# Merge-gate stores issued from GpSimd's queue instead of ScalarE's while attention runs: a hybrid attention and RG-LRU block

## The chip, the cores and the metric

The kernel runs on one core of a Trainium2 chip. The metric is the device time of one execution in microseconds (us); a set of runs is given by its median. The engines are named as in the profile: PE (TensorE), PEld (its weight loads), DVE (VectorE), ACT (ScalarE), POOL (GpSimd) and SP (SyncE, which only issues DMAs here).

## The reference

One decoder block on 1,024 tokens of width 1,024, in float32. An input projection is cut into the inputs of two branches and their gates; each branch is projected back, and two sigmoid gates (`m_attn`, `m_rnn`) merge them:

```python
mod = c @ w_ada[l] + b_ada[l]
shift, scale, gate = jnp.split(mod, 3, axis=-1)
h = rmsnorm(x, norm_g[l]) * (1.0 + scale[:, None, :]) + shift[:, None, :]
proj = h @ w_in[l]
q, k, v, g_attn, xr, g_rnn, m_attn, m_rnn = jnp.split(proj, SPLIT_POINTS, axis=-1)
q = partial_rope(q.reshape(B, S, N_HEADS, HEAD_DIM), positions)
k = partial_rope(k.reshape(B, S, N_KV_HEADS, HEAD_DIM), positions)
v = v.reshape(B, S, N_KV_HEADS, HEAD_DIM)
y_attn = sliding_window_attention_with_sinks(q, k, v, attn_sinks[l]) * jax.nn.silu(g_attn)
xr = causal_depthwise_conv(xr, conv_w[l], conv_b[l])
y_rnn = rg_lru(xr, positions, rg_wa[l], rg_ba[l], rg_wx[l], rg_bx[l], rg_lambda[l]) * jax.nn.silu(g_rnn)
merged = (jax.nn.sigmoid(m_attn) * (y_attn @ w_attn_proj[l])
          + jax.nn.sigmoid(m_rnn) * (y_rnn @ w_rnn_proj[l]))
x = x + gate[:, None, :] * (merged @ w_out[l])
return rmsnorm(x, final_g)
```

The attention has 16 query heads, 4 key heads, a window of 128 and a learned sink per head. The kernel makes each sigmoid as (tanh(z/2) + 1)/2, so what it stores of a merge gate is a tanh.

## The kernel before, in words

**Number format.** Every float32 matrix is split into a high part (rounded to fp32r, a cast on ACT, line 102) and the rest (a subtraction on DVE, line 108); a product is three matmuls: high by high, low by high, high by low.

**The input projection.** It is done in *pairs* of 128-column chunks (class `Pair`), each with seven block products instead of eight (a Strassen-like scheme). A product is 12 matmuls on a bank of PSUM (line 672, tiles `bk`), and fills one *slot* of the hand-written order. `Pair.place` puts every accompanying step into a slot: weight loads (`r<-w_main` by SP), casts (ACT), sums and rests (DVE), and the *sinks*, which take a result block to its place. The list `pairs` ends with the four pairs `MR`, the columns of `m_rnn`. Their sinks come from `tanh_sinks` (lines 768 to 787): ACT takes the tanh of a 128x512 block into a buffer of tag `c` (five of them, line 775), and the buffer is stored to the DRAM tensor `smr_d`, 256 KB a store. `MA`, the columns of `m_attn`, goes the same way to `sma_d`, long before attention.

**Attention over the last pair.** `N_ATT = 1`: when the last pair but one has been placed, `W["att"]` is set (line 1532) and the loop of lines 1563 to 1604 begins. Its round u handles a quarter group of heads for 128 queries, in 32 rounds and three to drain. In PE's order a round is `scores(u)` (8 matmuls into the one buffer `s_ps`, line 1216), then a *piece* (`piece()`: the 12 matmuls of one projection slot while pairs last, 12 matmuls `rp` of the recurrent branch's projection, line 171, afterwards), then `values(u-3)` (line 1288, `pv`, four matmuls, or two where no mask is needed) and `transposed(u-2)` (line 1254, `pt`). ACT copies the scores out of PSUM (line 1224), takes four exponentials (line 1240), does the piece's casts and tanhs, then copies `ob` (lines 1297, 1298) and casts `phc` (line 1259). DVE overlays the masked part (line 1230, which also reads `s_ps` for the last time), takes the maxima (line 1235), scales (lines 1246, 1247), does the piece's rests and joins (lines 108, 732, 743), joins the values (lines 1308, 1309, tile `yq`), and makes `plc` (line 1265). GpSimd issues the loads `dv` and `vs` (line 1195 on), copies the sinks (line 1204) and masks `phc` and `plc` into `phm` and `plm` (line 1274). Line 1433 (tile `al`) writes the low part of the gated attention result into memory that earlier buffers, the `c` buffers among them, held.

**What sets the order.** From line 183 to line 1620 (`order.close()`) all five engines run in the order in which the code is written. Behind that a planner orders the end (the attention projection from line 1652 on, the merge, the output projection) by its own costs. Between engines, the framework places the semaphore waits. Two of its habits matter here: the DMAs issued by SP and by ACT take turns, in the order of the program, on eight completion semaphores, and a DMA whose turn falls on a semaphore waits, on the engine that issues it, until the DMA that used it before (eight such DMAs earlier, by either engine) has landed; GpSimd's DMAs take turns on eight semaphores of their own.

**Stores by other engines.** `store` (line 757) puts a store off to the end of the pieces while `W["att"]` is set and gives it to SP; the merge gates' stores of line 777 do not pass through it.

Of the kernel before, what the change touches and what calls it, by code (L numbers as in the profile page):

```python
# [48 lines left out]
SL = [slice(0, HALF), slice(HALF, S)]  # L49
# [3 lines left out]
def tile_hybrid_block(ctx, tc, x, x_t, pk, rows, posr, posi, c_row, w_ss, w_gate, w_main, w_v,  # L53
                      w_g, w_ap, w_rp, w_out, out):
    nc = tc.nc
    V, A, G, T = nc.vector, nc.scalar, nc.gpsimd, nc.tensor

    def dma(dst, src, eng=nc.sync):
        dst, src = (a.bitcast(F32) if a.dtype == F32R else a for a in (dst, src))
        return eng.dma_start(dst, src)  # L60
# [497 lines left out]
    W = {}  # L558
# [18 lines left out]
    def blk(w=HALF):  # L577
        return stp.tile([P, HALF], F32, tag="c", name="c", bufs=5)[:, :w]
# [178 lines left out]
    def store(dst, src):  # L757

        if "att" in W:
            behind.append(lambda: dma(dst, src))  # L760
        else:
            dma(dst, src)
# [5 lines left out]
    def tanh_sinks(dst, silu):  # L768
        def steps(j, th):
            def sink(s):  # L770
                t = {}

                def f1():
                    t["t"] = blk()
                    A.activation(t["t"], s(), AF.Tanh, scale=0.5)  # L775
                    if not silu:
                        dma(dst[j][:, SL[th]], t["t"], A if "att" in W else nc.sync)

                def f2():
                    V.scalar_tensor_tensor(out=t["t"], in0=t["t"], scalar=1.0, in1=s(),  # L780
                                           op0=ALU.add, op1=ALU.mult)
                    store(dst[j][:, SL[th]], t["t"])

                return [("A", 0.62, 0, f1)] + ([("D", 0, 0.69, f2)] if silu else [])
            return sink
        return {"C11": steps(0, 0), "C12": (blk, steps(0, 1)), "C21": steps(1, 0),
                "C22": (blk, steps(1, 1))}
# [874 lines left out]
    for c in range(KC):  # L1662
# [11 lines left out]
        t = tpool.tile([P, S], F32, tag="tt", name="tt", bufs=2)  # L1674
# [175 lines left out]
```

## Time and profile before

| What | Value |
|---|---|
| Median of three runs | 932.46 us (929.82, 932.46, 933.45) |
| The profiled execution | 932.08 us |
| Its span, first to last instruction | 929.9 us |
| Mean granted TensorE clock | 0.998 |
| Busy: PE, DVE, ACT, POOL | 901.1, 681.1, 533.2, 85.5 us |
| DMA moved | 168.39 MB, mean 181 GB/s |

Times in the profile's rows are microseconds from the start of the span, durations of one instruction are in us in the timeline and in ns where a group is summed up. A row of the timeline gives the start, the duration, engine, line, operation, output and inputs; the bracket at its end gives the engine's idle time just before and what released it. Instructions that only issue a DMA (engine names with a q: ACTq, SPq) do not count as busy time, except on POOL, whose DMAs are shown with the time that GpSimd spends on them. PE's instructions overlap, so what PE loses is read from start to start.

### The profile page before, as it was taken

The page shows a single profiled execution, that of the slowest core. Times are in us where ns is not written, and L with a number is a line of the kernel's source. Part 1 is how long each engine was busy: PE and PEld are TensorE (multiplying, and loading weights), DVE is VectorE, ACT ScalarE, POOL GpSimd, SP SyncE. Part 2 cuts the span into 40 slices and gives each one's busy share as a digit, 9 for nine tenths or more (in the row PEclk, how much of TensorE's full clock was granted, in tenths as well). Part 3 has the DMA queues.
Part 4 walks back from the last instruction along what each step waited for, and adds up shares of the span by engine and source line. Part 5 has one row for each costly group of instructions (what it writes and reads, how often), then busy time and mean ns, then how long its engine had stood idle before and what let it go on. Part 6 is the DMA issues. An engine that isn't in the chain of part 4 may idle for free.

```text
span 929.9 us, 12279 instructions
## 1 busy us (share of the span) xinstructions
PE 901.1 (97%) x4217; PEld 745.5 (80%) x4217; DVE 681.1 (73%) x1042; ACT 533.2 (57%) x1026; POOL 85.5 (9%) x146
## 2 busy tenths in 40 slices
PE   3999999999999999999999999999999999999997
PEld 1679888887888888888887887788888888888886
DVE  5986888888769964996677675799999737657422
ACT  5643655454567656775596784788888622213211
POOL 0110000000000000000000001354454300000000
PEclk9999999999999999999999999999999999999999
DMA  9952548862332541444145349897656186536311
GB/s 350 414 187 102 194 152 281 304 232 85 114 110 94 180 161 36 145 164 154 57 141 187 99 173 294 298 335 219 221 178 189 57 317 219 163 123 242 136 68 68
DMA packets 82148, 168.39 MB, mean 181 GB/s; under 512 B 12756, under 2 KB 29140, under 8 KB 82087
## 3 DMA queue, kind: packets, MB, share of 16 engines
q1 hardware_dynamic: 78596, 159.47, 50.0%
q0 software_dynamic: 2192, 6.00, 1.9%
q10 hardware_dynamic: 1298, 2.15, 0.6%
q8 instruction: 33, 0.54, 0.3%
q14 instruction: 29, 0.23, 0.1%
HBM read 118.20 MB, written 49.78 MB: 181 GB/s over the span
## 4 chain that ended last, share of the span: by engine, by line
PE 87%; DVE 7%; DMA 3%; issue 1%; ACT 1%; SPq 0%; POOL 0%; ACTq 0%; DVEq 0%
PE bk L672 43%; PE rp L171 12%; PE pmain L171 6%; PE rp L1713 5%; PE pgate L966 5%; PE pmain L1713 4%; PE bk L171 3%; PE s_ps L1216 2%; PE pv L1288 2%; DVE jk L248 1%; PE pt L1254 1%; DMA wada<-w_ss 1%; DMA ks<-k_d 1%; PE bk L1461 1%; PE bk L1460 1%
## 5 line engine op out<-in xcount | busy, mean ns | idle before, releaser
L672 PE MATMUL bk<-nh,wl 128*128 128x512 f32 x352 | 137.3, 390 | 0.4 <-DVE wl L108 0.4
L672 PE MATMUL bk<-nh,wh 128*128 128x512 f32 x352 | 137.1, 389 | 0.0
L672 PE MATMUL bk<-nl,wh 128*128 128x512 f32 x352 | 137.0, 389 | 0.0
L108 DVE TENSOR_TENSOR wl<-r,wh 128x512 fp32r<-128x512 f32 x109 | 78.6, 727 | 20.3 <-ACT wh L102 20.3
L102 ACT CAST wh<-r 128x512 fp32r<-128x512 f32 x109 | 66.9, 618 | 43.4 <-PE bk L1461 11.6
L672 PEld LDWEIGHTS bk<-nh,wl 128*128 128x128 f32 x352 | 66.1, 188 | 15.1 <-DVE wl L108 1.4
L672 PEld LDWEIGHTS bk<-nh,wh 128*128 128x128 f32 x352 | 66.1, 188 | 13.7
L672 PEld LDWEIGHTS bk<-nl,wh 128*128 128x128 f32 x352 | 66.1, 188 | 13.6
L672 PE MATMUL bk<-hh,wl 128*128 128x512 f32 x176 | 68.6, 390 | 0.0
L672 PE MATMUL bk<-hh,wh 128*128 128x512 f32 x176 | 68.6, 390 | 0.0
L672 PE MATMUL bk<-hl,wh 128*128 128x512 f32 x176 | 68.5, 389 | 0.0
L108 DVE TENSOR_TENSOR wl<-ws,wh 128x512 fp32r<-128x512 f32 x76 | 51.4, 681 | 0.5 <-ACT wh L102 0.5
L1240 ACT ACTIVATE p<-p,small 128x129 f32<-128x129 f32 x128 | 50.1, 402 | 0.0
L102 ACT CAST wh<-ws 128x512 fp32r<-128x512 f32 x76 | 45.8, 614 | 5.4 <-DMA hla<-yl_d 3.7
L60 POOL DMA_DIRECT2D yh_d<-yh x1 | 0.6, 560 | 493.2 <-ACT yh L1033 493.2
L1730 ACT ACTIVATE o<-xo 128x1024 f32<-128x1024 f32 (+2 forms) x10 | 8.9, 889 | 53.2 <-DVE xo L1729 53.2
L672 PEld LDWEIGHTS bk<-hh,wh 128*128 128x128 f32 x176 | 33.0, 188 | 7.6 <-ACT wh L102 0.9
L1216 PE MATMUL s_ps<-ks,qs 128*128 128x256 f32 (+1 forms) x256 | 37.6, 289 | 1.5 <-DVE p L1230 1.4
L672 PEld LDWEIGHTS bk<-hh,wl 128*128 128x128 f32 x176 | 33.0, 188 | 7.0 <-DVE wl L108 0.3
L672 PEld LDWEIGHTS bk<-hl,wh 128*128 128x128 f32 x176 | 33.0, 188 | 6.9
L775 ACT ACTIVATE c<-bk 128x512 f32<-128x512 f32 x29 | 17.3, 598 | 29.9 <-PE bk L672 29.9
L672 PE MATMUL bk<-hha,wl 128*128 128x512 f32 x88 | 34.3, 390 | 0.1
(380 smaller groups left out, 2271.4 us busy)
## 6 DMA issues: line engine op xcount, KB each, us to landing
r<-w_main SPq DMA_DIRECT2D x100, 256.0 KB, 4.2
wada<-w_ss SPq DMA_DIRECT2D x16, 512.5 KB, 8.9
qs<-q_d SPq DMA_DIRECT2D x16, 512.0 KB, 5.8
ks<-k_d SPq DMA_DIRECT2D x24, 192.0 KB, 4.0
xT<-x_t SPq DMA_DIRECT2D x8, 512.0 KB, 9.0
q_d<-rhi SPq DMA_DIRECT2D x16, 256.0 KB, 4.0
q_d<-rlo SPq DMA_DIRECT2D x16, 256.0 KB, 3.9
sma_d<-c SPq DMA_DIRECT2D x16, 256.0 KB, 2.5
```

What stands on the lines that cost most here:

```text
L102: A.copy(dst[0][:], src)
L108: V.tensor_tensor(out=dst[1][:], in0=src, in1=f32(dst[0][:]), op=ALU.subtract)
L171: mm = T.matmul(ps[hf], ww, xx[kc][hf], start=(kc == 0 and ww is w_h and xx is xh), stop=(kc == KC - 1 and xx is xl))
L248: V.scalar_tensor_tensor(out=jk[:], in0=wada[kc, a][:], scalar=1.0, in1=c_bc[:], op0=ALU.mult, op1=ALU.mult, accum_out=mods[:, a * 8 + kc: ...
L672: W["pe"] = T.matmul(ps, ww[:, c], b[kc][xx_], start=(first and kc == 0 and i == 0), stop=(kc == 3 and i == 2), skip_group_check=not first)
L775: A.activation(t["t"], s(), AF.Tanh, scale=0.5)
L966: W["pe"] = T.matmul(ps[:, SL[hf]], ww[:, c0:c0 + P], xx_[:, SL[hf]], start=(ic == 0 and i == 0), stop=(ic == 1 and i == 2))
L1216: W["pe"] = T.matmul(o, qs[:, j, qc], ks[:, b, k0 + (0 if n else P):k0 + 256], start=(b == 0), stop=(b == 1))
L1240: A.activation(px[:, j, :], px[:, j, :], AF.Exp, bias=sm[:, 0, j:j + 1], accum_out=sm[:, 1, j:j + 1])
L1254: W["pe"] = T.transpose(pt[:, j, :], px[:, j, 0:P], ident[:])
L1288: W["pe"] = T.matmul(pv[:], b, m[:].rearrange("p j q -> p (j q)"), start=(i == 0), stop=(i == len(prods) - 1))
L1713: T.matmul(ps[:, sl], lhs[k][th][:, ts_], w[:, sl], start=(k == 0 and w is h_ and lhs is mh), stop=(k == KC - 1 and lhs is ml))
```

## The change

The tanh of a merge gate is stored by GpSimd's queue where it was stored by ScalarE's; that is, for blocks whose sink runs while `W["att"]` is set. Stores outside of attention stay with SP, and the other sinks are as they were.

```diff
                     t["t"] = blk()
                     A.activation(t["t"], s(), AF.Tanh, scale=0.5)
                     if not silu:
-                        dma(dst[j][:, SL[th]], t["t"], A if "att" in W else nc.sync)
+                        dma(dst[j][:, SL[th]], t["t"], G if "att" in W else nc.sync)
```

## The prediction

> **What bounds the kernel now.** I read the busy time by stretch first, since a mean over 930 us hides the stage that the change touches. A row gives the stretch, its length, then busy time and instructions of PE, PEld, DVE, ACT and POOL, the granted clock, the share of DMA and GB/s.
>
> ```profile
> 300.00:560.00 260.00, 259.60 (x1144) 214.15 (x1143) 198.33 (x252) 183.29 (x252) 1.10 (x2) 1.00 0.40 136
> 560.00:624.00 64.00, 60.28 (x315) 49.19 (x314) 46.89 (x85) 43.20 (x137) 22.21 (x37) 1.00 0.94 305
> 624.00:900.00 276.00, 275.86 (x1342) 231.52 (x1341) 190.91 (x294) 132.06 (x360) 53.31 (x87) 1.00 0.55 185
> ```
>
> PE is the bound from 300 to 560 and from 624 to 900 us. Only between them, where attention starts while the last projection pair runs, does it stand idle (3.7 of 64 us). Exactly there lie the stores that move, by the list of DMA issues and the answer for the DMA line on ACT:
>
> ```profile
> smr_d<-c SPq DMA_DIRECT2D x9, 256.0 KB, 2.0
> smr_d<-c ACTq DMA_DIRECT2D x7, 256.0 KB, 6.3
> dv<-dv_d POOLq DMA_DIRECT2D x16, 128.0 KB, 5.3
> L60 ACTq DMA_DIRECT2D smr_d<-c x7: 326/332/384, 560.1 to 603.7; - x7
> ```
>
> Seven of the 16 stores of `smr_d` are on ACT, from 560.1 to 603.7 us, 332 ns each. But ACT pays more than the issue. Its timeline around the third and fourth:
>
> ```profile
> 573.00 0.58 ACT L775 ACTIVATE c<-bk 128x512 f32<-128x512 f32 x1
> 576.89 0.33 ACTq L60 DMA_DIRECT2D smr_d<-c  x1
> 577.26 0.62 ACT L102 CAST wh<-ws 128x512 fp32r<-128x512 f32 x1 [3.68 <-DMA hla<-yl_d]
> 577.78 0.58 ACT L1224 COPY p<-s_ps 128x512 f32<-128x512 f32 x1
> ...
> 581.28 0.59 ACT L1224 COPY p<-s_ps 128x512 f32<-128x512 f32 x1
> ...
> 583.82 0.60 ACT L775 ACTIVATE c<-bk 128x512 f32<-128x512 f32 x1
> 587.02 0.33 ACTq L60 DMA_DIRECT2D smr_d<-c  x1
> 587.44 0.37 ACT L1297 COPY ob<-pv 64x256 f32<-64x256 f32 x1 [3.02 <-DMA r<-w_rp]
> ```
>
> The tanh of the third store ends at 573.58, its DMA goes out at 576.89: 3.31 us in which ACT stands still until the landing of `hla`, a load that has nothing to do with it. The fourth waits 2.60 us (584.42 to 587.02) for a load of `w_rp`. That is the framework's turn on the eight semaphores that SP and ACT share: the store's turn falls on one whose load is in flight. SP suffers the reverse, by its waits:
>
> ```profile
> SPq L60 <- DMA smr_d<-c: 6.6, 2, 5.8
> ```
>
> The chain that ended last runs through this turn-taking: a `ks` load, a `w_rp` load that waits for its semaphore, then ACT's store.
>
> ```profile
> 570.95 9.04 DMA ks<-k_d
> 580.01 6.93 DMA r<-w_rp
> ...
> 587.02 0.33 ACTq L60
> ```
>
> What PE loses by it stands in its own timeline, from one round's first score to the next:
>
> ```profile
> 569.81 1.12 PE L1216 MATMUL s_ps<-ks,qs 128*128 128x256 f32 x8
> 573.51 1.12 PE L1216 MATMUL s_ps<-ks,qs 128*128 128x256 f32 x8
> ...
> 577.21 0.60 PE L1254 MATMUL pt<-ident,p 128*128 128x128 f32 x4
> 579.18 1.22 PE L1216 MATMUL s_ps<-ks,qs 128*128 128x256 f32 x8 [1.37 <-DVE p L1230]
> ...
> 583.66 0.60 PE L1254 MATMUL pt<-ident,p 128*128 128x128 f32 x4
> 584.02 1.19 PE L1216 MATMUL s_ps<-ks,qs 128*128 128x256 f32 x8
> ...
> 589.18 0.47 PE L1288 MATMUL pv<-phc,vs 128*128 128x512 f32 x1 [1.23 <-ACT phc L1259]
> ...
> 591.25 1.20 PE L1216 MATMUL s_ps<-ks,qs 128*128 128x256 f32 x8
> ...
> 596.59 1.20 PE L1216 MATMUL s_ps<-ks,qs 128*128 128x256 f32 x8
> ...
> 602.23 1.20 PE L1216 MATMUL s_ps<-ks,qs 128*128 128x256 f32 x8
> ...
> 608.35 1.09 PE L1216 MATMUL s_ps<-ks,qs 128*128 128x128 f32 x8
> ...
> 618.76 1.21 PE L1216 MATMUL s_ps<-ks,qs 128*128 128x256 f32 x8
> ```
> ```profile
> 623.81 1.19 PE L1216 MATMUL s_ps<-ks,qs 128*128 128x256 f32 x8
> ```
>
> The last full round, 618.76 to 623.81, takes 5.05 us; I take that as the price of a full round. A round without values and transposes takes 573.51 - 569.81 = 3.70, the transposes 584.02 - 583.66 = 0.36, so four value matmuls cost 0.99, two about 0.50. Against these the rounds that start at 573.51, 579.18, 584.02, 591.25, 596.59 and 602.23 lose 1.61, 0.28, 2.18, 0.29, 0.59 and 1.07 us, the two from 608.35 to 618.76 together 0.31. The sum is 6.33 us: it is more than the idle time of the window, because matmuls that follow a pause also start farther apart. It is also the most that this change can give, since PE loses nothing behind it.
>
> **The change part by part.** (1) *ACT loses seven issues and two waits.* Without the third store the cast starts at 573.6 and ends its turn 0.52 later (577.26 to 577.78). The next copy of scores then waits only for PE's scores (573.51 + 1.12), so it runs at 574.7 instead of 577.78. DVE had waited for it:
>
> ```profile
> 578.40 0.73 DVE L1230 COPY_PREDICATED p<-mgt,s_ps 128x512 f32<-128x512 uint32 x1 [3.87 <-ACT p L1224]
> ...
> 588.22 0.42 DVE L1308 TENSOR_TENSOR yq<-pv,ob 64x256 f32<-64x256 f32 x1 [3.25 <-ACT ob L1298]
> ...
> 598.80 0.42 DVE L1308 TENSOR_TENSOR yq<-pv,ob 64x256 f32<-64x256 f32 x1 [0.61 <-ACT ob L1298]
> ...
> 604.93 0.42 DVE L1308 TENSOR_TENSOR yq<-pv,ob 64x256 f32<-64x256 f32 x1 [1.08 <-ACT ob L1298]
> ...
> 610.76 0.68 DVE L1433 TENSOR_TENSOR al<-yq,ah 128x512 fp32r<-128x512 f32 x1
> ```
>
> The overlay of 578.40 comes at 575.3, and PE's next scores start behind its own transposes, at 577.21 + 0.36 = 577.57: 1.61 gained. The round after starts at 577.57 + 3.70 + 0.36 + 0.50 = 582.13: 1.89 gained. ACT's work from the copy at 581.28 to the tanh's end at 584.42 is 3.14 us without a gap; that copy now waits for the scores that start at 577.57 and take 1.12, so it runs at 578.7, the tanh ends at 581.8 and, with no store behind it, `ob` follows when PE's two value matmuls are out (577.57 + 3.70 + 0.50 = 581.8, and some 0.2 until the last has ended), at 582.0. That is 5.4 us before 587.44. `phc` is done by 583.4, long before PE wants it (582.13 + 3.70 = 585.8): the wait of 1.23 goes, and the next round starts at 582.13 + 5.05 = 587.18, 4.07 gained.
>
> (2) *DVE is next late.* From 588.22 until the overlay that lets PE's scores of 618.76 start, DVE works almost without a pause: 30.5 us, 1.7 of them waits for `ob` (the rows 598.80 and 604.93). That lateness made the losses of the later rounds (0.29, 0.59, 1.07, 0.31). It now starts 5.4 us earlier, at 582.8, and its 28.8 us of work end at 611.6. PE needs 587.18 + 5 x 5.05 = 612.43. So PE is the bound again, with 0.8 us to spare, and the whole 6.33 us come back.
>
> (3) *GpSimd gains seven issues.* Their nearest price is its own `dv` and `vs` loads:
>
> ```profile
> 595.79 0.56 POOL L60 DMA_DIRECT2D dv<-dv_d  x1
> ...
> 605.58 0.64 POOL L1274 TENSOR_SCALAR_AFFINE_SELECT phm<-phc 128x512 fp32r<-128x512 f32 x1 [2.85 <-ACT phc L1259]
> ```
>
> Seven by 0.56 are 3.9 us, in a window where POOL is busy 22 of 64 us. A store waits on GpSimd for its tanh; queued behind it are a sink copy and the masks `phm` and `plm` of the same round, sometimes `dv` and `vs`. The masks wait for `phc`, which ACT makes after the tanh and after two `ob` copies, so the store is out before (the row 605.58 shows 2.85 us of rest). Taken at nothing; if every one of the last four held PE by its full length it were 2.2 us, and a gain is excluded, since nothing leaves POOL.
>
> (4) *SP.* The wait of 5.8 us for a store that held the loads at 560 goes; what follows it (`w_rp`, `hha`) goes out some 5 us earlier. Worth nothing by itself, since PE waits for no load here; it is the cover for (1), which needs the loads up to 6 us sooner.
>
> (5) *The landing.* `al` writes where `c` buffers were and so waits for the stores. Before, the sixth store's tanh ended by 602.5 and `al` ran 8.3 us later without a wait. In the new order about 7.6 us lie between. The landings bound a store on GpSimd at 5.3 (the `dv` median) to 8.3 (ACT's store was in by then), so DVE waits 0 to 0.7; I take 0.3, as the ACT median of 6.3 is nearer to nothing.
>
> The sum: 6.33 - 0.3 = 6.0 us. The profiled execution took 932.08, so 926.1; the median of the runs shown lies 0.38 above that execution, so 926.5 us, 0.64% less. About 0.5% (4.7 us) is what a measurement of this kernel can tell from no change.
>
> **The rivals.** *Only the waits' share comes back.* DMA is busy 94% of the window at 305 GB/s. To do the same bytes in 58 us it must carry 336. If loads or DVE hold the later rounds, the 4.07 us of (1) are left, or 3 if a score load is a microsecond late: 928.4 to 929.5. For it: landings of 7 to 9 us. Against: SP starts 5 us earlier, and DVE has 0.8 us to spare.
>
> *Only the issue time is saved.* The turn-taking might put an equal wait somewhere else on the path; left is 7 x 0.332 = 2.3 us of ACT: 930.2. Against: ACT then has no DMA that can wait, and GpSimd takes turns on other semaphores, with few DMAs. The Trainium skill, page "DMA: Bandwidth & Descriptors", section "Issuing engines are not separate DMA queues", says that issuing from several engines saves only the sequencer's time, usually little against the DMA: by it this rival would be the forecast. The trace disagrees: the seven issues take 2.3 us, the two waits ahead of them 5.9.
>
> *Slower: the end is planned anew.* The planner orders what is behind line 1620, and its picture of the queues changes. PE is busy there without a gap, and each `w_ap` load that is exposed costs its landing:
>
> ```profile
> r<-w_ap SPq DMA_DIRECT2D x16, 256.0 KB, 5.4
> ```
>
> Two exposed (10.8 us) outweigh the gain: 932.5 - 6.0 + 10.8 = 937.3. From two on it decides. Against: 275.86 busy of 276, and no instruction there is touched.
>
> *It does nothing*: seven stores may have moved with PE's losses remaining, 932.5, if the waits were only put down to the wrong releaser. Against: SP and ACT show the same turn-taking from both sides.
>
> **How the numbers follow.** The forecast gets 0.57, the waits' share alone 0.25, the issue time 0.08, nothing 0.05, slower 0.05. The range goes from all 6.33 us and the 1.5 us by which runs differ, about 924.8, to the issue-time rival, 930.3. Faster by over 0.5% is nearly all of the forecast, 0.56; within 0.5% the middle cases, 0.39; slower 0.05.
>
> **What would show it.** Right: no `smr_d` issue on ACT, seven on POOL of about 0.56 us; no wait of ACT of over 2 us between 570 and 590; score starts at 577.6, 582.1 and 587.2 where 579.18, 584.02 and 591.25 stood, and 5.05 us apart from then on; the window's PE idle under 1 us; SP's wait for `smr_d` gone. Wrong: PE waiting for a load (`ks`, `hh`) or for `plm`, DVE waiting ahead of `al`, or gaps after 740 us.

## The result and the profile after

| | before | after | ratio, 95% interval |
|---|---|---|---|
| first comparison, median of 5 runs each | 930.26 us (929.62 to 933.45) | 926.40 us (925.69 to 926.77) | 0.9946 (0.9932 to 0.9960) |
| second comparison, 9 and 5 runs | 931.46 us (930.18 to 932.65) | 927.48 us (927.11 to 929.65) | 0.9962 (0.9948 to 0.9975) |
| profiled execution | 932.08 us, span 929.9 | 926.55 us, span 924.8 | |

The kernel is faster, by 0.54% in the first comparison and 0.38% in the second; the medians differ by 3.9 and 4.0 us, the first two profiled executions by 5.5. (The ratios are those on record with their intervals; the quotients of the two medians are 0.9959 and 0.9957.) Executions at a granted clock of 0.66 to 0.85 are left out of every median, ratio and table of this document. Of the 5.5 us, 0.4 lie outside the profiled span: the time is 2.1 to 2.2 us longer than the span in every run of the kernel before, and 1.7 to 1.8 in every run of the kernel after. No run shows why, and the prediction has no term for it. The forecast of 926.5 us met the level; the gain that it worked out, 6.0 us, was too large. Where the difference went is the subject of what follows.

The window of attention over the last pair, after, with the same columns as before, and behind it the stretch up to 900 us:

```profile
560.00:624.00 64.00, 63.81 (x350) 54.49 (x349) 52.65 (x95) 48.31 (x152) 26.37 (x48) 1.00 0.98 337
624.00:900.00 276.00, 275.44 (x1330) 230.62 (x1329) 187.27 (x288) 128.30 (x347) 51.30 (x83) 1.00 0.53 177
```

PE's idle time in the window went from 3.72 to 0.19 us, and DMA now carries 337 GB/s there (305 before). But behind the window, where PE had idled 0.14 us of 276, it now idles 0.56. The stores, in the tile's own answer:

```profile
L60 POOL DMA_DIRECT2D smr_d<-c x7: 539/547/570, 566.7 to 598.6; - x7
```

All seven are on GpSimd, at 547 ns. ACT's timeline at the places where it had stood still:

```profile
573.42 0.61 ACT L102 CAST wh<-ws 128x512 fp32r<-128x512 f32 x1
...
574.60 0.59 ACT L1224 COPY p<-s_ps 128x512 f32<-128x512 f32 x1 [0.57 <-PE s_ps L1216]
...
581.33 0.59 ACT L775 ACTIVATE c<-bk 128x512 f32<-128x512 f32 x1
581.94 0.37 ACT L1297 COPY ob<-pv 64x256 f32<-64x256 f32 x1
```

The cast that had to wait until 577.26 for a store's turn runs at 573.42, and `ob` follows the fourth tanh at once, at 581.94 (587.44 before). PE's rounds answer to it:

```profile
577.50 1.19 PE L1216 MATMUL s_ps<-ks,qs 128*128 128x256 f32 x8
...
582.09 1.19 PE L1216 MATMUL s_ps<-ks,qs 128*128 128x256 f32 x8
...
587.13 1.19 PE L1216 MATMUL s_ps<-ks,qs 128*128 128x256 f32 x8
...
597.23 1.19 PE L1216 MATMUL s_ps<-ks,qs 128*128 128x256 f32 x8
...
602.56 1.09 PE L1216 MATMUL s_ps<-ks,qs 128*128 128x128 f32 x8
...
613.01 1.21 PE L1216 MATMUL s_ps<-ks,qs 128*128 128x256 f32 x8 [0.16 <-DVE p L1230]
```

The first three starts stood at 579.18, 584.02 and 591.25 before. Two losses are left: 0.28 us in the round from 597.23 (5.33 us instead of 5.05) and 0.35 in the two from 602.56 (10.45 instead of 10.10). DVE's timeline tells whose they are:

```profile
582.72 0.42 DVE L1308 TENSOR_TENSOR yq<-pv,ob 64x256 f32<-64x256 f32 x1 [0.37 <-ACT ob L1298]
...
593.45 0.42 DVE L1308 TENSOR_TENSOR yq<-pv,ob 64x256 f32<-64x256 f32 x1 [0.61 <-ACT ob L1298]
...
599.14 0.41 DVE L1308 TENSOR_TENSOR yq<-pv,ob 64x256 f32<-64x256 f32 x1 [0.65 <-ACT ob L1298]
...
605.02 0.68 DVE L1433 TENSOR_TENSOR al<-yq,ah 128x512 fp32r<-128x512 f32 x1
...
612.24 0.72 DVE L1230 COPY_PREDICATED p<-mgt,s_ps 128x512 f32<-128x512 uint32 x1
```

DVE starts its dense stretch at 582.72, as worked out (582.8), but the overlay that releases the eleventh round ends at 612.96 and not at 611.6: the two waits for `ob`, 0.61 and 0.65 us, are still there. ACT is late with `ob` in these rounds because it first waits for DVE's join of the piece, and then has a copy or a tanh of it to do:

```profile
592.07 0.58 ACT L721 COPY u<-bk 128x512 f32<-128x512 f32 x1 [0.62 <-DVE c L732]
...
597.71 0.63 ACT L775 ACTIVATE c<-u 128x512 f32<-128x512 f32 x1 [0.60 <-DVE u L743]
```

So the two engines wait for each other in the order as it is written, and an earlier start does not remove that. The loss of 0.28 us in the round from 597.23 hangs on the same: GpSimd makes `plm` when DVE's `plc` is there, which comes behind the second late `ob`, and PE's matmul on `plm` starts at 601.87, 0.41 us behind the one before it (0.23 in the next rounds):

```profile
600.80 1.02 POOL L1274 TENSOR_SCALAR_AFFINE_SELECT plm<-plc 128x512 fp32r<-128x512 f32 x1 [0.36 <-DVE plc L1265]
```

`al` waits for no store.

The table below follows PE through the traces of this study: from the third score start of attention (573.45 us in the kernel after) to the eleventh (613.01), from there to the last (717.53), and from that to the start of the last matmul (918.07). All are differences of two rows of PE's timeline.

| kernel | 3rd to 11th | 11th to last | last to end |
|---|---|---|---|
| before | 45.25 | 104.49 | 199.88 |
| before, second trace | 43.98 | 104.49 | 200.12 |
| after | 39.56 | 104.52 | 200.54 |
| after, second trace | 39.57 | 106.55 | 199.86 |
| stores 1 and 2 alone on GpSimd | 40.97 | 104.48 | 200.88 |
| stores 3 and 4 alone on GpSimd | 42.35 | 104.54 | 200.98 |
| issue time put back on ACT | 40.01 | 104.49 | 199.95 |
| waits put back on ACT | 43.93 | 104.50 | 199.83 |
| `hha`, `hla` loads on GpSimd | 44.20 | 104.49 | 199.87 |
| stores on SP | 39.57 | 108.29 | 199.86 |
| after, cast in halves | 39.58 | 104.77 | 199.86 |
| the same, second trace | 39.57 | 105.29 | 199.91 |

The first column is what the change does; the other two show what is given back.

### The profile page after: what moved, and what is told of

It is laid out like the page before. It is cut to its first block, busy times and chain, and to the rows that moved or that the text cites. A ratio compares the mean times of both kernels' runs of the same rounds, so it can differ in the third digit from the quotient of the medians.

```text
span 924.8 us, 12289 instructions
## 1 busy us (share of the span) xinstructions
PE 900.3 (97%) x4217; PEld 747.5 (81%) x4217; DVE 681.3 (74%) x1042; ACT 533.0 (58%) x1026; POOL 87.6 (9%) x153
## 4 chain that ended last, share of the span: by engine, by line
PE 83%; DVE 7%; DMA 5%; issue 2%; ACT 1%; SPq 0%; POOL 0%; DVEq 0%; ACTq 0%
PE bk L672 44%; PE rp L171 9%; PE pgate L966 5%; PE bk L171 4%; PE rp L1713 4%; PE pmain L1713 4%; PE s_ps L1216 3%; PE pmain L171 3%; PE pv L1288 2%; DMA tt<-tr_d 2%; DMA wo<-w_out 1%; PE pt L1254 1%; DMA wada<-w_ss 1%; PE bk L1461 1%; PE bk L1460 1%
```

## The experiments

The *turn theory* is the prediction's: ACT's two waits for a shared completion semaphore are the price, and they went. Its rivals: the *issue theory* (ACT's seven issues of 0.332 us are what counts) and the *loads theory* (SP, freed of its own wait for a store, sends loads sooner). That the turn has eight places shows in the rows of the first trace of the kernel before: the `w_rp` load of 580.01 is the eighth DMA of SP and ACT behind the first `ks` load of 570.95, ACT's store of 587.02 is the eighth behind that `w_rp` load, and each went out when the earlier one had landed.

**Waits put back.** Behind the third and fourth tanh ACT copies a tile onto itself, with the stores on GpSimd as in the kernel after:

```diff
+                        n = W["st"] = W.get("st", 0) + ("att" in W)
+                        for _ in range({3: 5, 4: 4}.get(n, 0)):
+                            A.copy(t["t"], t["t"])
```

> The kernel after, with copies of the block onto itself put on ACT behind the tanh of the third store (five, about 3 us) and of the fourth (four, about 2.4 us), so that ACT is held as long as it was by its waits, while GpSimd issues the stores and SP is free. Turn theory: ACT's hold alone brings back PE's losses of 1.6 and 2.2 us and some of DVE's lateness: 3 to 6 us slower than the kernel after, at most 1.5 us better than before. Loads theory: the loads stay early, so within 1 us of the kernel after. Issue theory: within 1 us of the kernel after.

Measured: 930.72 us, ratio to before 0.9998 (0.9984 to 1.0011). The rows come from another execution of this kernel, of 931.10 us; what was expected of them:

> A second look at the kernel after with copies on ScalarE behind the third and fourth tanh (five and four copies of 128x512, some 3.0 and 2.4 us), for a trace of it; its time is known (a ratio to before of 0.9998). It computes the same. Turn theory: TensorE loses in the same places as in the kernel before, with scores starting near 579, 584 and 591 us, and the distance from the third to the eleventh score round is 44 to 46 us, where the kernel before had 45.25 and the kernel after 39.56, although no store stands on ScalarE and SyncE's loads go out as early as in the kernel after. Loads or issue theory: those starts stay within 1 us of the kernel after, and the lost time lies elsewhere.

ACT's timeline (lines behind 777 have numbers 3 higher in this kernel):

```profile
574.49 3.23 ACT L779 COPY c<-c 128x512 f32<-128x512 f32 x5
...
584.81 2.58 ACT L779 COPY c<-c 128x512 f32<-128x512 f32 x4
```

and PE's:

```profile
579.53 1.22 PE L1219 MATMUL s_ps<-ks,qs 128*128 128x256 f32 x8 [0.84 <-DVE p L1233]
...
584.40 1.19 PE L1219 MATMUL s_ps<-ks,qs 128*128 128x256 f32 x8
...
591.39 1.19 PE L1219 MATMUL s_ps<-ks,qs 128*128 128x256 f32 x8
```

With 3.23 and 2.58 us of pure standing still, these rounds start 5.2, 10.0 and 17.0 us behind the third one (574.38); in the kernel before it was 5.7, 10.5 and 17.7, in the kernel after 4.1, 8.6 and 13.7. As a time the whole gain is gone, although GpSimd issues the stores as in the kernel after, SP's next `w_rp` loads go out as early (2.14 us behind the third round's start, 2.15 there) and PE waits for no load. The first column, 43.93, lies just below the expected 44 to 46: of the 5.69 us that it differs by in the first two traces, 4.37 are back, not all. Loads and issue theory fall here as the main cause.

**Issue time put back.** A copy of 128 columns on ACT (0.30 us) in place of each of the seven issues (0.33):

```diff
+                        if "att" in W:
+                            A.copy(t["t"][:, :128], t["t"][:, :128])
```

> The kernel after, with a copy of 128 columns of the tanh (about 0.3 us, the length of one DMA issue on ScalarE) put on ScalarE behind each of the seven tanhs. So ScalarE gets back the issue time that the change took from it, and none of the waits. It computes the same. Issue theory (what counted were seven times 0.332 us on ScalarE): some 2.3 us or more come back, 928.5 to 929.5 us, a ratio to the kernel before of 0.997 or above. Turn theory (what counted were the waits for a shared semaphore ahead of the third and fourth store, and ScalarE has rest for 0.3 us a round): at most 0.8 us come back, 926.2 to 927.3 us, ratio 0.994 to 0.996, and the score starts stay at 577.5, 582.1 and 587.1 us within 0.4 us.

Measured: 927.81 us (926.24 to 928.40), ratio 0.9952 (0.9934 to 0.9970). The score starts are 577.38, 581.96 and 587.00 us, and the first column has 40.01 instead of 39.56: issue time is worth 0.45 us of the 5.69. The median is 0.5 us over what the turn theory expected, inside the spread of the kernel after itself (925.69 to 929.65).

**Two halves of the change.** First only stores 1 and 2 on GpSimd, then, with `(3, 4)` in place of `(1, 2)`, only 3 and 4 (the cut is against the kernel before):

```diff
-                        dma(dst[j][:, SL[th]], t["t"], A if "att" in W else nc.sync)
+                        n = W["st"] = W.get("st", 0) + ("att" in W)
+                        dma(dst[j][:, SL[th]], t["t"], (G if n in (1, 2) else A) if "att" in W else nc.sync)
```

> Only the first and the second store go to GpSimd; the third and fourth stay on ACT. Loads theory: SP's wait of 5.8 us is gone and with it nearly the whole loss, 5 us less. Turn theory: SP's loads go out some 5 us earlier; the third store's turn now falls behind a load that has landed by then, so ACT's first wait shrinks to under 0.5 us; the fourth store's turn is behind a load of w_rp, which goes out some 4 us earlier, so that a wait between 0 and 2 us is left: 2 to 5 us less than before. Issue theory: 0.7 us less.

Measured: 929.20 us, ratio 0.9969 (0.9957 to 0.9981). ACT's timeline (lines from 777 on are 1 higher here):

```profile
573.10 0.58 ACT L775 ACTIVATE c<-bk 128x512 f32<-128x512 f32 x1
575.05 0.34 ACTq L60 DMA_DIRECT2D smr_d<-c  x1
...
582.00 0.59 ACT L775 ACTIVATE c<-bk 128x512 f32<-128x512 f32 x1
582.82 0.35 ACTq L60 DMA_DIRECT2D smr_d<-c  x1
```

The waits ahead of the third and fourth store shrink to 1.37 and 0.23 us (3.31 and 2.60 before), though these two stores stand where they stood: with the first two gone from the shared turns, others carry them. (The first of these waits was expected under 0.5 us.) Since SP is also free of its own wait for the first store here, this run does not part the turn theory from the loads theory. 4.28 us are won by the eleventh round, of which 1.0 is given back at the end (third column).

> Only the third and the fourth store of the attention stage go to GpSimd; the other five stay on ACT. Turn theory (ACT's two waits of 3.3 and 2.6 us for its turn on a semaphore that a load in flight holds are what costs): both waits are gone though SP still stands 5 to 6 us for the first store; score starts near 577.5, 582.1, 587.1 as in the kernel after; 4 to 5.5 us less than before, 0.4 to 0.6%. Issue theory (the seven issues of 0.33 us on ACT cost): two sevenths of 2.3 us, 0.7 us less. Loads theory (SP's wait for the first store makes the loads late, and that costs): no gain, within 0.5 us of before.

Measured: 929.02 us, ratio 0.9983 (0.9969 to 0.9998), where 0.994 to 0.996 was expected. The rows come from another execution; what was expected of them:

> A second look at the kernel in which only the third and the fourth store go out from GpSimd, for a trace of it; its time is known (a ratio of 0.9983 to the kernel before, where 0.994 to 0.996 was expected). Turn theory: the score starts of the third to fifth round come near 577.5, 582.1 and 587.1 us as in the kernel after, and a wait of over 1 us for a foreign load stands on ScalarE ahead of one of the fifth to seventh stores, which are still there and whose turns now fall on other loads. Loads theory (SyncE still waits for the first two stores and sends its loads late): TensorE waits for ks, qs or a w_rp load somewhere between 575 and 610 us, and ScalarE has no such wait. Third possibility: neither, the starts to 724 us come as in the kernel after, and the gain is lost behind 840 us.

It took 930.75 us; ACT's timeline, and PE's behind it:

```profile
591.04 0.62 ACT L775 ACTIVATE c<-c 128x512 f32<-128x512 f32 x1
594.32 0.33 ACTq L60 DMA_DIRECT2D smr_d<-c  x1
594.68 0.58 ACT L721 COPY u<-bk 128x512 f32<-128x512 f32 x1 [3.02 <-DMA hl<-yl_d]
```
```profile
592.39 1.20 PE L1217 MATMUL s_ps<-ks,qs 128*128 128x256 f32 x8
595.32 0.74 PE L171 MATMUL rp<-hha,wh 128*128 128x512 f32 x2 [1.73 <-ACT u L721]
...
599.49 0.72 PE L1217 MATMUL s_ps<-ks,qs 128*128 128x256 f32 x4
```

The third to fifth rounds start at 577.72, 582.31 and 587.35, as in the kernel after. Then the fifth store, still on ACT, waits 2.66 us (591.66 to 594.32) for a load of `hl`, and the round from 592.39 takes 7.10 us. The wait has moved to the next store whose turn is bad: the miss speaks for the turn theory, and against moving the two stores that happen to wait.

**Other loads moved instead.** The stores stay on ACT; the loads `hha` and `hla`, one of which the third store had waited for, go out from GpSimd:

```diff
-                dma(hs[i], yh_d[c][:, SL[i]])
-                dma(ls[i], yl_d[c][:, SL[i]])
+                dma(hs[i], yh_d[c][:, SL[i]], G)
+                dma(ls[i], yl_d[c][:, SL[i]], G)
```

> All seven stores stay on ACT as before; instead the eight loads hha and hla (256 KB each) are issued by GpSimd, so the eight shared turns reach further back and the third store's turn falls behind a load of qs issued at about 566. Turn theory: ACT's wait ahead of the third store is under 0.5 us and ahead of the fourth under 1 us, although ACT issues every store: 3 to 5.5 us less than before. Issue theory: no gain. A theory by which GpSimd's queue as such is better for the stores: no gain, or slower by the 4.5 us that GpSimd spends on eight more issues.

Measured: 930.63 us, ratio 0.9997 (0.9986 to 1.0008). ACT's timeline:

```profile
572.85 0.59 ACT L775 ACTIVATE c<-bk 128x512 f32<-128x512 f32 x1
573.47 0.35 ACTq L60 DMA_DIRECT2D smr_d<-c  x1
...
581.20 0.59 ACT L775 ACTIVATE c<-bk 128x512 f32<-128x512 f32 x1
585.88 0.33 ACTq L60 DMA_DIRECT2D smr_d<-c  x1
586.30 0.37 ACT L1297 COPY ob<-pv 64x256 f32<-64x256 f32 x1 [4.51 <-DMA r<-w_rp]
```

The third store, with its turn shifted, goes out at once, as expected; the fourth, expected to wait under 1 us, now waits 4.09 us for a `w_rp` load. So the wait belongs to the turn and not to the store. The expected net gain did not come, since the new wait is longer than the old one, and PE waited 1.57 us for a `qs` load besides.

**Stores on SP.** The same seven stores issued by SP, in their places (against the kernel before):

```diff
-                        dma(dst[j][:, SL[th]], t["t"], A if "att" in W else nc.sync)
+                        dma(dst[j][:, SL[th]], t["t"])
```

> The seven stores go out from SyncE's queue at the places where they stood, neither from ScalarE's nor from GpSimd's. ScalarE then has neither their issues nor their waits, but SyncE issues in order: each load behind a store waits for that store's tanh. It computes the same. Turn theory: ScalarE's two waits are gone and the score starts of the third to fifth round stay within 1 us of the kernel after (577.5, 582.1, 587.1), unless a load that stands behind a store comes late; 926 to 929 us, some 3 to 6 us below the kernel before. Loads theory (what the change brought was loads that SyncE sends 5 us sooner): SyncE now waits at each of the seven stores, so nothing is gained, 931 us or more. Issue theory: 2.3 us gained, 929.3 us.

Measured: 928.11 us, ratio 0.9971 (0.9959 to 0.9982). The trace is of the slowest of the seven executions, 929.94 us. PE's timeline after the attention window:

```profile
625.98 0.73 PE L171 MATMUL rp<-yh,wh 128*128 128x512 f32 x2 [0.83 <-DMA yh<-yh_d]
...
627.97 1.16 PE L171 MATMUL rp<-yl,wh 128*128 128x512 f32 x2 [0.80 <-DMA yl<-yl_d]
```

Up to the eleventh round it equals the kernel after (39.57); freeing ACT is all that this part needs. Then PE waits for `yh` and `yl`, and the second column loses 3.8 us (108.29). The waits are some 2 us of that; behind them, from 628.0 to 631.4 us, the granted clock was 0.51 (1.00 ahead of them), and the round ends another 1.7 us late.

**The kernel after once more, and its end.** In the first trace of the kernel after PE waits at 845 us, where it did not before. PE's and ACT's timelines, after:

```profile
844.33 3.90 ACT L1648 CAST wo<-wo 128x1024 fp32r<-128x1024 f32 x4 [3.51 <-issue]
...
845.44 0.73 PE L1713 MATMUL rp<-wo,hh 128*128 128x512 f32 x2 [0.43 <-ACT wo L1648]
```

The row sums up four casts, one of each weight tile; PE needs the first. In the kernel before that one begins at 849.32 and ends some 0.25 us ahead of PE's use, which stands at 850.63. To test whether the last 0.7 us are lost there, the cast was cut in halves:

```diff
-        A.copy(h_, w32[:])
+        for sl in SL: A.copy(h_[:, sl], w32[:, sl])
```

> The kernel after, with the rounding copy of each output weight tile w_out (128x1024, on ScalarE) done as two copies of half the columns, so that TensorE's first product with the left half can start half a copy sooner. It computes the same. End theory (0.65 us of the 5.7 us that were gained by the last score round are lost at 845 us, where TensorE waits 0.43 us for that copy): the wait shrinks to under 0.15 us, the distance from the last score round to the end of TensorE's work goes from 200.86 us back towards the 200.19 us of the kernel before, and the time is 0.3 to 0.7 us below the kernel after, about 925.8 us, ratio to before 0.9925 to 0.9945. Rival (the end is bound by its loads, and the copy is only the last link): the wait moves to another product of the end, and the time is that of the kernel after within 0.2 us.

Measured: 927.12 us (926.92 to 928.45), ratio 0.9961 (0.9949 to 0.9974). The distance to the end is 199.86 us, the time did not improve. So it was run again beside the unchanged kernel after:

> The kernel after with the rounding copy of each output weight tile in two halves, beside the unchanged kernel after on the same chip (in its first run the distance from the last score round to the last product was 200.14 us, where the kernel after had 200.82 and the kernel before 200.16, and the whole run began 0.8 us later for another reason). End theory: the same 0.7 us again in the trace, and a median 0.3 to 0.8 us below that of the kernel after run beside it. Rival: the traces agree and the times do not differ, since runs of the same kernel differ by as much as the 0.7 us.

> The kernel after once more, unchanged, beside the next kernel and the kernel before on one chip. If the gain is that of the first comparison: 926.0 to 927.0 us, a ratio to before of 0.993 to 0.996, and a spread of its own of about 1 us where that of before is 4 us, since it has no wait left whose length depends on when a load lands.

Measured: 926.43 us (926.01 to 927.40) with the cast in halves, ratio 0.9947 (0.9933 to 0.9960), against 927.48 us (927.11 to 929.65) without, ratio 0.9962 (0.9948 to 0.9975). The two traces of this pair do not put that difference at the cast: the last column is 199.91 and 199.86. What differs is the middle, 105.29 against 106.55, and that is a load. PE's timeline of the second trace of the kernel after:

```profile
626.44 0.73 PE L171 MATMUL rp<-yh,wh 128*128 128x512 f32 x2 [1.07 <-DMA yh<-yh_d]
...
628.06 0.73 PE L171 MATMUL rp<-yl,wh 128*128 128x512 f32 x2 [0.43 <-DMA yl<-yl_d]
```

The `yh` loads of this kernel in its first trace, and in the second (the issues, then landing times):

```profile
L60 SPq DMA_DIRECT2D yh<-yh_d x2: 319/326/333, 611.4 to 613.8; - x2
...
DMA to landing us min/median/max: 8.4/8.4/8.4
```
```profile
L60 SPq DMA_DIRECT2D yh<-yh_d x2: 319/326/333, 611.8 to 614.7; - x2
...
DMA to landing us min/median/max: 8.9/10.3/11.7
```

The second of them lands at 613.8 + 8.4 = 622.2 us in one execution and at 614.7 + 11.7 = 626.4 in the other; PE wants it at about 625.4. Over both batches the halved cast has a median of 927.01 us of 11 runs and the kernel after 926.94 of 10, so as a time the cast is worth nothing that these runs show. That it removes the wait at 845 us is not shown either: the unchanged kernel had none in its second trace. (The distances in these expectations are taken to the end of PE's work, by other rows than the table's.)

Where the last column's loss comes from, the traces at hand do show. The cast waits for DVE, which scales the tile, and DVE for the tile's load:

```profile
833.63 1.23 DVE L1645 TENSOR_TENSOR wo<-wo,gate_bc 128x1024 f32<-128x1024 f32 x1 [3.80 <-DMA wo<-w_out]
```

Counted from the last score start, the cast begins at 126.07 and 126.38 us in the two traces of the kernel before, at 126.80 and 125.90 in those of the kernel after, at 127.15 and 127.25 in those of the two halves of the change, each time 10.7 us behind this scaling. Up to 126.1 the last column is 199.8 to 199.9; behind that the column grows by about as much as the cast is late (127.25: 200.98). So the end is late where a load of `w_out` comes late, which differs between executions of one kernel, the kernel before included. The load goes out when DVE has finished a block that had waited for a load of `smr_d`; further back it was not followed. The halved cast met early loads (125.08 and 126.13).

Also wrong was the expectation that the kernel after spreads by only 1 us; it has a load left whose landing decides.

**The kernel before once more.**

> The kernel before once more, unchanged, for a second trace of it: its times spread from 929 to 934 us, those of the kernel after over little more than 1 us. Turn theory: the spread is that of the two waits on ScalarE, whose length is set by when hla and w_rp land. So the waits ahead of the third and fourth store have other lengths than the 3.3 and 2.6 us of the first trace, and the eleventh score start moves with them: if the run takes about 930 us, the score starts between 573 and 592 us lie some 2 us nearer to those of the kernel after. Rival (the spread is of the start or of the end): the waits are the same within 0.3 us, and the difference to the first trace lies ahead of 560 or behind 724 us.

It took 930.97 us. ACT's timeline:

```profile
572.93 0.58 ACT L775 ACTIVATE c<-bk 128x512 f32<-128x512 f32 x1
575.93 0.33 ACTq L60 DMA_DIRECT2D smr_d<-c  x1
...
582.87 0.60 ACT L775 ACTIVATE c<-bk 128x512 f32<-128x512 f32 x1
585.69 0.33 ACTq L60 DMA_DIRECT2D smr_d<-c  x1
```

The waits are 2.42 and 2.22 us here, 3.31 and 2.60 in the first trace: together 1.27 less, and the first column is 1.27 us shorter (43.98 against 45.25). The score starts lie 1.0 to 1.3 us nearer to those of the kernel after, not 2. Ahead of 560 us and behind 724 the two traces differ by 0.1 and 0.2 us. At least this part of the spread of the kernel before (929 to 936 us over all comparisons) is the length of these two waits.

## Why the prediction was right, and where it was not

*What bounds.* Right: the two waits of ACT are the main cause. Put back as plain copies they take the whole gain away as a time, and 4.37 of the 5.69 us of the first column; the seven issues put back take 0.45 of these. No run tells whose the remaining 0.87 us are. The Trainium skill, page "DMA: Bandwidth & Descriptors", section "Issuing engines are not separate DMA queues", says that another issuing engine saves only sequencer time; here the runs disagree, as the prediction had it: 0.45 us are that, 4.37 are waits.

*Step (1), ACT.* Right to 0.1 us: starts at 577.50, 582.09 and 587.13 against 577.57, 582.13 and 587.18, `ob` at 581.94 against 582.0.

*Step (2), DVE.* This step failed in part. "DVE has 0.8 us to spare" took its 1.7 us of waits for `ob` as consequences of the lateness; 1.26 of them stayed, because ACT waits for DVE's joins there. 28.8 us of work and 1.3 of waits from 582.72 end at 612.8, and the eleventh round starts at 613.01 instead of 612.43.

*Step (3), GpSimd.* Right at nothing. Behind the last two stores its masks still have rest, and the late `plm` (a sign of being wrong by the prediction) had waited for DVE, not for a store:

```profile
598.64 0.54 POOL L60 DMA_DIRECT2D smr_d<-c  x1 [0.66 <-ACT c L775]
599.17 0.20 POOL L1204 COPY p<-sink 128x4 f32<-128x4 f32 x1
599.80 0.63 POOL L1274 TENSOR_SCALAR_AFFINE_SELECT phm<-phc 128x512 fp32r<-128x512 f32 x1 [0.42 <-ACT phc L1259]
```

*Step (4), SP.* "Worth nothing by itself" held, "the cover for (1)" did not always: `yh` goes out 5.0 us sooner in the one trace and 4.1 in the other, while PE comes 5.7 sooner, and its landing takes 8.4 to 11.7 us. In the second trace this load is exposed. The prediction had that as the sign that it would be wrong (PE waiting for a load) and gave the loads a rival of its own, at 928.4 to 929.5; the run with the late load took 928.02. *Step (5), the landing*, was 0 where 0.3 was taken.

*The sum.* "PE loses nothing behind it" is the term that was mis-sized. The first column gives 5.69 us between the first two traces (6.33 were worked out, less 0.64, nearly all of it in the late rounds of step (2)). Against it stand 0.69 us behind the eleventh round in the one trace of the kernel after and 2.04 in the other (sums of the second and third column, 305.06 and 306.41 against 304.37). The second trace of the kernel before, with shorter waits, leaves 4.41 to gain. The mean of 5.69 and 4.41 less the mean of 0.69 and 2.04 is 3.7 us; with the 0.4 outside the span it is 4.1, near what the medians differ by, 3.9 and 4.0 (a rough reckoning from two traces each). So the 6.0 us were the gain over one execution whose waits were long, without the tail. The level came out at 926.4 because the base of three runs had its median at 932.46; over more runs it is 930.3 to 931.5. That the forecast met it is in part luck: a base that was 1 to 2 us high made up for a gain that was 2 us too large. (The foot of the range, 932.46 - 6.33 - 1.5, is 924.6, not 924.8.)

*The rivals.* Slower through a new plan of the end did not come: no load of `w_ap` is exposed. The end does take something back in some executions, by a cast that had 0.25 us to spare and waits for a load of `w_out`; the kernel before shows the same in its second trace, by 0.24 us.

## What to carry to other kernels

An engine that only issues a DMA can stand still for another engine's load if both take turns on the same completion semaphores; look for idle time whose releaser is a tensor that the instruction does not read. Move all such DMAs of the busy engine, not those that wait now: with two of seven moved the wait went to the fifth. And read such a gain from several executions: a wait for a landing is long in one and short in the next, and the loads behind it must come sooner by the whole gain or they take part of it back.

## What the runs showed of the hardware that was not expected

The second `yh` load (512 KB, 128x1024, float32) took 8.4 us to land in one execution of the kernel after and 11.7 in another, both with the DMA engines full (a share of 1.05 in the profile's windows from 614 to 624 us). With the `hha` and `hla` loads on GpSimd, a `w_rp` load of 256 KB held its turn for 4.1 us of ACT's time. GpSimd took 0.55 us for an issue for which ACT takes 0.33. Behind two waits of PE of 0.83 and 0.80 us, 2 us apart, the granted clock was 0.51 for 3.4 us (stores on SP); behind waits of 1.07 and 0.43 us in the second trace of the kernel after it stayed at 1.00.
